# A two-block transformer kernel: norms without GpSimd, and the second block's edges done stream by stream

## The chip, the cores and the metric

The kernel runs on one core of a Trainium2 chip. The metric is device time in microseconds (us), the median of several executions. A core has a matrix engine (TensorE, PE in the profile), three engines for elementwise work (VectorE or DVE, ScalarE or ACT, GpSimd or POOL) and a queue that issues transfers (SyncE or SP). Each engine executes its instructions in the order in which they were laid down when the kernel was built, and waits at an instruction until what it needs is there.

## The reference

Two blocks follow each other. The first works on 256 tokens of 1024 features: a gated FFN, an attention mixer, another gated FFN, each between two RMS norms. The second has two streams, the 256 tokens x and 256 context tokens xc, and two layers. All is float32. Cut to what matters:

```python
def rms_norm(x, g):
    return x * lax.rsqrt(jnp.mean(x * x, axis=-1, keepdims=True) + EPS) * g

def adaln_norm(x, g, shift, scale):
    return rms_norm(x, g) * (1 + scale) + shift

# first block
x = x + 0.5 * rmsnorm(swiglu(rmsnorm(x, ffn1_pre_g), ...), ffn1_post_g)
x = x + rmsnorm(mixer(rmsnorm(x, mix_pre_g)), mix_post_g)
x = x + 0.5 * rmsnorm(swiglu(rmsnorm(x, ffn2_pre_g), ...), ffn2_post_g)

# second block, layer l; mx and mc are six vectors each, from a small matmul (modulation)
h, hc = adaln_norm(x, norm1_g[l], mx[0], mx[1]), adaln_norm(xc, norm1_g[l], mc[0], mc[1])
# three branches (Fourier, window attention, gated scan) of h @ w_in[l] and hc @ w_in[l]
if not last:
    xc = xc + mc[2] * yc                  # yc = merged branches @ w_out[l]
    xc = xc + mc[5] * sq_relu_mlp(adaln_norm(xc, norm2_g[l], mc[3], mc[4]), w_ff1[l], w_ff2[l])
x = x + mx[2] * y
x = x + mx[5] * sq_relu_mlp(adaln_norm(x, norm2_g[l], mx[3], mx[4]), w_ff1[l], w_ff2[l])
```

In the last layer the context is needed only for keys, values and states, so only x has outputs there.

## The kernel before, in words

Features lie on partitions, eight tiles of 128, and tokens along the free axis. Each float32 operand of a matmul is split into a high and a low part, and each product is three matmuls (`mm3`, L239 to L242). A weight comes in units of 512 KB (`wunit`, L230): a DMA into `raw`, a cast on ScalarE for `hi` (L235), a subtraction on VectorE for `lo` (L236), with three buffers each. `linear` (L246) makes 256 output features from units of four input tiles. In the first block it is 256 tokens wide, so a unit feeds 24 matmuls of 256 columns; in the second block's layer 0 both streams go together in 512 columns.

A norm's sum of squares is gathered by `Sums` (L316): each output block is squared on ScalarE, the squares of the blocks but the last are added on GpSimd (L341), and matmuls with one column (`tok`, L323) sum over the features, for the added squares when the block before the last has come (L343 to L345), for the last one at the end. The row scales come from a few small steps (`rs_tok`, L360, a power on GpSimd) and are spread over all partitions by two diagonal tiles and two matmuls with them (`spread`, L369). `post_norm` (L421) scales the outputs and adds them to X, the second of four pairs on GpSimd (L437); `pre_norm` (L411) then splits X times gain into high and low parts (`gained`, L394) and makes the next sums. While a norm waits, PE does fillers: columns of the second block's gates for the context (`ctx_gate`, L702).

`adaln` (L448) is the norm of the second block. It takes both streams at once where there are two. For each of eight k: a multiplication on VectorE (L458), per stream an Identity with scale and bias on ScalarE for `hi` (L461) and a multiply-add on GpSimd (L462), and a subtraction on VectorE for `lo` (L465). It stands in the prologue for the context, beside FFN2 for the context, at the start of layer 0 for x, between w_out and ff1 of each layer, and between the layers.

In `layer` (L885) the two streams' outputs of w_out come block by block of 256 features, four blocks; `residual` adds them to x (L1335), the squares of the last block go in halves (`half`, L350). Then adaln, then ff1 in two halves of the hidden features, each followed by ff2. `mods` (L663), the modulation matmuls of layer 1 with their transfers of 1 MB, are handed out between these by `next(between)`. After the branches' projections, `hcol(0)` makes the first head's forget columns and its query and gate, `values` the value columns for both streams, `scan(0)` the first head's gated scan. The order on each engine is set by a scheduler at build time, which goes by priorities; nothing in it is written out by hand.

## Time and profile before

| | |
|---|---|
| median of three runs | 2115.73 us (2113.39 to 2123.27) |
| the profiled execution | 2119.52 us, span 2117.7 us |
| mean granted clock of TensorE | 0.985 |
| busy: PE, VectorE, ScalarE, GpSimd | 97%, 59%, 49%, 8% |

The times of one profiled execution are used throughout; it took 3.8 us more than the median. PE's busy time is the sum of its matmuls' durations, which overlap in a pipeline, so a busy PE is not PE at its peak: what a matmul takes is read from the distance of two starts, or from a count in a window. The granted clock of a window is 1.00 at full speed (2.4 GHz) and 0.50 at the lower level (1.2 GHz).

### The profile page before, as it was taken

The page shows a single profiled execution, that of the slowest core. Times are in us where ns is not written, and L with a number is a line of the kernel's source. Part 1 is how long each engine was busy: PE and PEld are TensorE (multiplying, and loading weights), DVE is VectorE, ACT ScalarE, POOL GpSimd, SP SyncE. Part 2 cuts the span into 40 slices and gives each one's busy share as a digit, 9 for nine tenths or more (in the row PEclk, how much of TensorE's full clock was granted, in tenths as well). Part 3 has the DMA queues.
Part 4 walks back from the last instruction along what each step waited for, and adds up shares of the span by engine and source line. Part 5 has one row for each costly group of instructions (what it writes and reads, how often), then busy time and mean ns, then how long its engine had stood idle before and what let it go on. Part 6 is the DMA issues. An engine that isn't in the chain of part 4 may idle for free.

```text
span 2117.7 us, 33603 instructions
## 1 busy us (share of the span) xinstructions
PE 2056.8 (97%) x13623; PEld 1795.5 (85%) x13623; DVE 1259.8 (59%) x1930; ACT 1047.0 (49%) x1692; POOL 159.6 (8%) x154
## 2 busy tenths in 40 slices
PE   8999999999999999999999999999999998998999
PEld 8899988999999777888776678778778778998998
DVE  5574666765557699855454442343267897666644
ACT  5353455544446688655343331233255776555532
POOL 1131110211220000000002000000120000001000
PEclk9999999999999999999999999999999999999999
DMA  7986564566552211168533663342233223654654
GB/s 231 304 241 188 174 169 131 158 186 181 173 194 81 70 40 50 53 223 273 193 131 106 212 225 129 110 149 90 86 104 90 61 63 108 211 178 143 187 186 135
DMA packets 284158, 318.57 MB, mean 150 GB/s; under 512 B 18528, under 2 KB 272306, under 8 KB 277346
## 3 DMA queue, kind: packets, MB, share of 16 engines
q1 hardware_dynamic: 284002, 316.42, 47.8%
q8 instruction: 107, 1.75, 0.3%
q14 instruction: 49, 0.40, 0.1%
HBM read 308.96 MB, written 11.35 MB: 151 GB/s over the span
## 4 chain that ended last, share of the span: by engine, by line
PE 89%; DVE 4%; ACT 4%; POOL 2%; issue 1%; DMA 1%; SPq 0%; POOLq 0%; DVEq 0%; ACTq 0%
PE mx L240 13%; PE mx L242 13%; PE mx L241 13%; PE mm L240 11%; PE mm L242 11%; PE mm L241 11%; PE hg L1168 2%; POOL sq L462 1%; PE ax L326 1%; PE mx L674 1%; PE ax L674 1%; PE at L1029 1%; PE at L1066 1%; DVE lo L236 1%; PE at L1056 1%
## 5 line engine op out<-in xcount | busy, mean ns | idle before, releaser
L236 DVE TENSOR_TENSOR lo<-raw,hi 128x1024 fp32r<-128x1024 f32 x460 | 563.5, 1226 | 564.3 <-ACT hi L235 558.2
L235 ACT CAST hi<-raw 128x1024 fp32r<-128x1024 f32 x460 | 478.3, 1040 | 742.9 <-PE mx L241 417.5
L240 PE MATMUL mx<-hh,hi 128*128 128x256 f32 (+1 forms) x1216 | 377.3, 310 | 4.3 <-ACT hh L461 3.0
L241 PE MATMUL mx<-hl,hi 128*128 128x256 f32 (+1 forms) x1216 | 374.8, 308 | 3.0 <-DVE hl L465 2.4
L242 PE MATMUL mx<-hh,lo 128*128 128x256 f32 (+1 forms) x1216 | 375.2, 309 | 1.7 <-DVE lo L236 1.7
L240 PE MATMUL mm<-hh,hi 128*128 128x256 f32 (+1 forms) x1096 | 363.6, 332 | 2.0 <-ACT z L1111 1.3
L242 PE MATMUL mm<-hh,lo 128*128 128x256 f32 (+1 forms) x1096 | 360.1, 329 | 0.0
L241 PE MATMUL mm<-hl,hi 128*128 128x256 f32 (+1 forms) x1096 | 358.1, 327 | 1.1 <-DVE hl L465 1.0
L240 PEld LDWEIGHTS mx<-hh,hi 128*128 128x128 f32 x1216 | 231.3, 190 | 29.8 <-ACT hi L235 6.7
L241 PEld LDWEIGHTS mx<-hl,hi 128*128 128x128 f32 x1216 | 232.2, 191 | 18.4 <-DVE hl L465 6.0
L242 PEld LDWEIGHTS mx<-hh,lo 128*128 128x128 f32 x1216 | 230.7, 190 | 13.2 <-DVE lo L236 1.9
L240 PEld LDWEIGHTS mm<-hh,hi 128*128 128x128 f32 x1096 | 208.8, 191 | 28.1 <-issue 5.8
L241 PEld LDWEIGHTS mm<-hl,hi 128*128 128x128 f32 x1096 | 209.3, 191 | 18.9 <-issue 2.5
L242 PEld LDWEIGHTS mm<-hh,lo 128*128 128x128 f32 x1096 | 208.3, 190 | 16.8 <-issue 2.3
L240 PE MATMUL mx<-fh,hi 128*128 128x512 f32 (+1 forms) x288 | 100.3, 348 | 0.0
L241 PE MATMUL mx<-fl,hi 128*128 128x512 f32 (+1 forms) x288 | 100.2, 348 | 0.0
L242 PE MATMUL mx<-fh,lo 128*128 128x512 f32 (+1 forms) x288 | 100.0, 347 | 0.0
L341 POOL TENSOR_TENSOR acc<-sq 128x512 f32<-128x512 f32 x12 | 20.3, 1690 | 872.9 <-ACT sq L331 872.9
L242 PE MATMUL mm<-fh,lo 128*128 128x256 f32 (+1 forms) x224 | 74.7, 333 | 0.0
L240 PE MATMUL mm<-fh,hi 128*128 128x256 f32 (+1 forms) x224 | 74.3, 332 | 0.0
L241 PE MATMUL mm<-fl,hi 128*128 128x256 f32 (+1 forms) x224 | 74.1, 331 | 0.0
L242 PE MATMUL mx<-hidh,lo 128*128 128x256 f32 x220 | 62.4, 283 | 0.7 <-DVE lo L236 0.7
(373 smaller groups left out, 3864.5 us busy)
## 6 DMA issues: line engine op xcount, KB each, us to landing
raw<-in_w_ff_dram SPq DMA_DIRECT2D x128, 512.0 KB
raw<-in_w_in_dram SPq DMA_DIRECT2D x124, 512.0 KB
wm<-in_w_mod_dram SPq DMA_DIRECT2D x48, 1024.0 KB
raw<-in_ffn_w_gate_dram SPq DMA_DIRECT2D x44, 512.0 KB
raw<-in_ffn_w_up_dram SPq DMA_DIRECT2D x44, 512.0 KB
raw<-in_ffn_w_down_dram SPq DMA_DIRECT2D x40, 512.0 KB
raw<-in_w_qkv_dram SPq DMA_DIRECT2D x24, 512.0 KB
raw<-in_w_out_dram SPq DMA_DIRECT2D x24, 512.0 KB
```

Of the source, the lines that this page charges most:

```text
L235: S.copy(hi, raw)
L236: V.tensor_tensor(out=lo, in0=raw, in1=hi.bitcast(F32), op=ALU.subtract)
L240: PE.matmul(ps, l[0], r[0], start=start, stop=False)
L241: PE.matmul(ps, l[0], r[1], start=False, stop=False)
L242: return PE.matmul(ps, l[1], r[0], start=False, stop=stop)
L326: PE.matmul(self.ss[:, t:t + 1], sq[:, i * T + t * P:i * T + (t + 1) * P], ones[:, :1], start=(first and i == 0 and t == 0), stop=(last an ...
L462: nc.gpsimd.tensor_scalar(out=xs, in0=xs, scalar1=A[s][:, k:k + 1], scalar2=B[s][:, k:k + 1], op0=ALU.mult, op1=ALU.add)
L674: PE.matmul(ps[32 * c:32 * c + 32, :], cst_[:, k, :], wm[:, c * 512:(c + 1) * 512], start=(k == 0), stop=(k == KD - 1), tile_position=(0, ...
L1029: PE.matmul(scs[t], q[e][:, t * P:(t + 1) * P], kd[g][i][:, 512 - nk:], start=(i == 0), stop=(i == 1 and s == 1))
L1056: PE.transpose(pt[:, kt * T + t * P:kt * T + (t + 1) * P], sb[:, c0:c0 + P], ident)
L1066: mm = PE.matmul(op[e * 64:e * 64 + 64, :T], vt[:, vc:vc + 64], pts[e][:, kt * T:(kt + 1) * T], start=(ki == 0), stop=(ki == nk // P - 1))
L1168: PE.matmul(ps[:, (s * 2 + st) * P:(s * 2 + st + 1) * P], kt[:, s * T + st * P:s * T + (st + 1) * P], qt[:, s * T + tt * P:s * T + (tt + 1 ...
```

## The change

Four things are changed.

- **Sums.** The additions of squares go to VectorE, and the one-column matmuls for the added squares are issued with the last block (in `half`, with its first half). The second pair's addition to X in `post_norm` goes to VectorE too.
- **Gained inputs.** `post_norm` can make the next norm's gained parts right after each pair of X.
- **adaln.** It goes stream by stream inside k: VectorE multiplies x by the scale and the row factor, ScalarE adds the bias for `hi`, VectorE adds the bias and subtracts `hi` for `lo`. GpSimd keeps the power of the row scales.
- **Streams.** In layer 0, blocks 2 and 3 of w_out are done for the context, then for x, each followed by its adaln; the first two blocks of ff1 in the same way; so is the last block of the second ff2, followed by layer 1's adaln of that stream. Layer 1 starts with the context's part of the first head's forget columns and the context's values (`values1`), then x's part and x's values. Weight units that are used for each stream apart are fetched, cast and split twice: 18 units more.

```diff
     class Sums:
...
                 elif self.j < self.n - 1:
                     acc = tmp(512, "acc", 2) if self.j == 1 else self.acc
-                    nc.gpsimd.tensor_tensor(out=acc, in0=self.acc, in1=sq, op=ALU.add)
+                    V.tensor_tensor(out=acc, in0=self.acc, in1=sq, op=ALU.add)
                     self.acc = acc
-                if self.j == self.n - 2:
+                if self.j == self.n - 1:
                     self.ss = ax_tile()
                     self.tok(self.acc, True, False)
-                if self.j == self.n - 1:
                     self.tok(sq, False, True)
...
             S.activation(sq, src, AF.Square)
+            if i == 0:
+                self.ss = ax_tile()
+                self.tok(self.acc, True, False)
...
-    def pre_norm(g, ss=None):
-
-        units = [gained(lambda i: X[:, 2 * j + i, 0, :], g + 2 * j, *pair(j)) for j in range(4)]
+    def gained_x(g, j):
+        return gained(lambda i: X[:, 2 * j + i, 0, :], g + 2 * j, *pair(j))
...
-    def post_norm(pss, g, factor, fill=()):
+    def post_norm(pss, g, factor, fill=(), then=None):
...
                 V.tensor_tensor(out=two(hs[j]), in0=two(hs[j]), in1=twice(rs), op=ALU.mult)
-                (nc.gpsimd if j == 1 else V).tensor_tensor(out=xpair(j), in0=two(hs[j]), in1=xpair(j), op=ALU.add)
+                V.tensor_tensor(out=xpair(j), in0=two(hs[j]), in1=xpair(j), op=ALU.add)
+                if then is not None:
+                    units.append(gained_x(then, j))
+        return units
...
         for k in range(KD):
-            hi, lo = units[k]
-            xn = tmp(512, "sq", 3)[:, c]
-            V.tensor_tensor(out=xn, in0=x[:, k, s0:s1, :].rearrange("p s t -> p (s t)"), in1=ps[:, c], op=ALU.mult)
             for s in streams:
-                xs = xn[:, (s - s0) * T:(s - s0 + 1) * T]
-                S.activation(hi[:, s * T - at:(s + 1) * T - at], xs, AF.Identity, scale=A[s][:, k:k + 1], bias=B[s][:, k:k + 1])
-                nc.gpsimd.tensor_scalar(out=xs, in0=xs, scalar1=A[s][:, k:k + 1], scalar2=B[s][:, k:k + 1],
-                                        op0=ALU.mult, op1=ALU.add)
-            cu = slice(s0 * T - at, s1 * T - at)
-            V.tensor_tensor(out=lo[:, cu], in0=xn, in1=hi[:, cu].bitcast(F32), op=ALU.subtract)
+                hi, lo = (u[:, s * T - at:(s + 1) * T - at] for u in units[k])
+                u = tmp(512, "sq", 3)[:, :T]
+                V.scalar_tensor_tensor(out=u, in0=x[:, k, s, :], scalar=A[s][:, k:k + 1], in1=ps[:, s * T:(s + 1) * T],
+                                       op0=ALU.mult, op1=ALU.mult)
+                S.activation(hi, u, AF.Identity, bias=B[s][:, k:k + 1])
+                V.scalar_tensor_tensor(out=lo, in0=u, scalar=B[s][:, k:k + 1], in1=hi.bitcast(F32),
+                                       op0=ALU.add, op1=ALU.subtract)
...
+        def values1(s):
+
+            for b in range(2):
+                if s == 1:
+                    vh.append([None, None])
+                [ps] = linear_tok(w_in, 0, KD, C_I + b * 256, of(hboth, s), T)
+                vh[b][s] = ut("vh", 4)
+                V.tensor_copy(vh[b][s], ps)
...
-        hcol(0)
-        values()
+        if last:
+
+            early = [linear128(w_in, c, hboth, 512, ((1, "at"),)) for c in (C_FF, C_FB)]
+            values1(1)
+            hcol(0, early)
+            values1(0)
+        else:
+            hcol(0)
+            values()
...
-        for jb in range(4):
+
+        for jb in range(4 if last else 2):
             residual(linear(a["w_out_2"][l], 0, KD, jb * 256, mact, ntok), jb, 2, sums)
+        if not last:
+            h = mh
+            for s in (1, 0):
+                for jb in (2, 3):
+                    [ps] = linear(a["w_out_2"][l], 0, KD, jb * 256, of(mact, s), T)
+                    residual1(ps, jb, 2, s, sums)
+                adaln(x, (s,), A2, B2, h, sums)
...
-            for j in range(n_h):
+            if hf == 0 and not last:
...
+                for s in (1, 0):
+                    for j in range(2):
+                        [ps] = linear(a["w_ff1_2"][l], 0, KD, j * 256, of(hboth, s), T)
+                        next(between, None)
...
-            for jb in range(4):
+            for jb in range(4 if last or hf == 0 else 3):
                 residual(linear(a["w_ff2_2"][l], hf * kh * P, kh, jb * 256, fact, ntok), jb, 5,
                          sums if hf == ns - 1 else None)
...
+            h1 = [pair(k) for k in range(KD)]
+            for s in (1, 0):
+                [ps] = linear(a["w_ff2_2"][l], kh * P, kh, 3 * 256, of(fact, s), T)
+                residual1(ps, 3, 5, s, sums)
+                adaln(x, (s,), [derived[l + 1][q][0] for q in range(2)], [modt[l + 1][:, q, 0:8] for q in range(2)], h1, sums)
```

`residual1` does for one stream what `residual` does for both, and `of(act, s)` takes a stream's columns of the operands.

How this moves instructions is seen at three places. The first is the end of FFN1 on PE, where the down projection's third block ends. In a row the names are output, stationary and moving operand, then the tile; `ax` is the tile of the sum, `acc` the added squares, `hid` the hidden features. Before:

```order
L241 MATMUL mx<-hidl,hi 128x256
L242 MATMUL mx<-hidh,lo 128x256
L326 MATMUL ax<-cmain,acc 128x1 x4
L240 MATMUL mx<-hidh,hi 128x256
L241 MATMUL mx<-hidl,hi 128x256
```

And now, at the end of the fourth block, with the filler (`hch`, `hcl`, the context's parts) behind it:

```order
L242 MATMUL mx<-hidh,lo 128x256
L326 MATMUL ax<-cmain,acc 128x1 x4
L240 MATMUL mm<-hch,hi 128x256
L241 MATMUL mm<-hcl,hi 128x256
L242 MATMUL mm<-hch,lo 128x256
```

The matmuls that read the added squares moved behind the fourth block, 114 rows later on PE.

The second place is PE between w_out and ff1 of layer 0. `sq` is the last block's square, `wm` a modulation weight, `diag` the diagonal tile, `hh` and `hl` the norm's high and low parts. Before:

```order
L242 MATMUL mx<-hh,lo 128x512
L355 MATMUL ax<-cmain,sq 128x1 x4
L674 MATMUL mx<-wm,csil_12035 32x512 x5
L355 MATMUL ax<-cmain,sq 128x1 x4
L674 MATMUL mx<-wm,csil_12035 32x512 x3
L379 MATMUL ax<-diag,cmain 128x128 x4
L240 MATMUL mx<-hh,hi 128x512
L240 MATMUL mm<-hh,hi 128x512
L674 MATMUL mx<-wm,csil_12035 32x512
L241 MATMUL mx<-hl,hi 128x512
```

And now the context's spread, between two matmuls of w_out's blocks for x:

```order
L240 MATMUL mm<-hh,hi 128x256
L241 MATMUL mm<-hl,hi 128x256
L381 MATMUL ax<-diag,cmain 128x128 x2
L242 MATMUL mm<-hh,lo 128x256
L240 MATMUL mm<-hh,hi 128x256
```

The matmuls with the diagonals no longer stand right ahead of the first matmul that reads the norm's output; the other stream's matmuls lie around them.

The third place is VectorE at the same edge. `big` is the residual x, `rvs` the row sums, `der` and `modt` the scale and the shift. Before:

```order
L236 TENSOR_TENSOR lo<-raw,hi 128x1024 x2
L1335 SCALAR_TENSOR_TENSOR big<-mm,modt_139,big 128x256 x2
L1335 SCALAR_TENSOR_TENSOR big<-mx,modt_139,big 128x256 x2
L236 TENSOR_TENSOR lo<-raw,hi 128x1024
L363 TENSOR_SCALAR rvs<-ax 128x2 x2
L376 TENSOR_SCALAR diag<-cmain,rss 128x128 x2
L458 TENSOR_TENSOR sq<-big,ax 128x512 x3
L465 TENSOR_TENSOR hl<-sq,hh 128x512
L458 TENSOR_TENSOR sq<-big,ax 128x512
L465 TENSOR_TENSOR hl<-sq,hh 128x512 x2
```

And now, for the context, up to x's turn:

```order
L365 TENSOR_SCALAR rvs<-ax 128x2
L378 TENSOR_SCALAR diag<-cmain,rss 128x128
L469 SCALAR_TENSOR_TENSOR sq<-big,der_144,ax 128x256 x3
L472 SCALAR_TENSOR_TENSOR hl<-sq,modt_139,hh 128x256 x3
L469 SCALAR_TENSOR_TENSOR sq<-big,der_144,ax 128x256 x3
L1374 SCALAR_TENSOR_TENSOR big<-mm,modt_139,big 128x256
L472 SCALAR_TENSOR_TENSOR hl<-sq,modt_139,hh 128x256 x3
L469 SCALAR_TENSOR_TENSOR sq<-big,der_144,ax 128x256 x2
L1374 SCALAR_TENSOR_TENSOR big<-mm,modt_139,big 128x256
L236 TENSOR_TENSOR lo<-raw,hi 128x1024
L472 SCALAR_TENSOR_TENSOR hl<-sq,modt_139,hh 128x256 x2
L341 TENSOR_TENSOR acc<-acc,sq 128x512
```

The norm's steps come in threes for one stream, with x's residuals, a weight's low part and an addition of squares between them.

## Rows read from the trace of the kernel before

**Rows 1.** Page: busy time and share of each engine; traffic in 40 slices, GB/s

```profile
PE 2056.8 (97%) x13623; PEld 1795.5 (85%) x13623; DVE 1259.8 (59%) x1930; ACT 1047.0 (49%) x1692; POOL 159.6 (8%) x154
...
GB/s 231 304 241 188 174 169 131 158 186 181 173 194 81 70 40 50 53 223 273 193 131 106 212 225 129 110 149 90 86 104 90 61 63 108 211 178 143 187 186 135
```

**Rows 2.** Page: the chain of work that ended last, by engine

```profile
PE 89%; DVE 4%; ACT 4%; POOL 2%; issue 1%; DMA 1%; SPq 0%; POOLq 0%; DVEq 0%; ACTq 0%
```

**Rows 3.** PE's waits over the span: us in total, times, longest

```profile
PE ax L326 <- POOL acc L341: 7.7, 6, 1.5
...
PE ax L379 <- DVE diag L376: 3.6, 5, 1.4
...
PE mx L240 <- ACT hh L461: 3.0, 2, 1.9
...
PE mx L241 <- DVE hl L465: 2.4, 4, 1.0
...
PE mx L242 <- DVE lo L236: 2.3, 2, 1.7
...
PE at L240 <- ACT hh L461: 1.9, 1, 1.9
...
PE ax L355 <- ACT sq L353: 1.4, 1, 1.4
```

**Rows 4.** Nine windows: engines' busy us (instructions), granted clock, DMA share, GB/s

```profile
209.09:212.50 3.41, 3.41 (x17) 3.41 (x18) 0.29 (x1) 1.04 (x1) 0.00 (x0) 0.50 0.27 75
...
1134.10:1140.93 6.83, 6.83 (x23) 5.77 (x23) 0.00 (x0) 0.00 (x0) 0.40 (x1) 0.50 0.17 60
...
1919.17:1929.41 10.24, 7.45 (x31) 6.87 (x32) 6.23 (x17) 4.88 (x9) 5.88 (x9) 0.50 0.18 53
sum 51.20, PE 47.58 PEld 43.28 DVE 17.00 ACT 14.22 POOL 16.49; mean PE 5.29 PEld 4.81 DVE 1.89 ACT 1.58 POOL 1.83
```

**Rows 5.** Timeline, 205.5 to 210 us: start, duration, instruction

```profile
206.68 1.75 POOL L341 TENSOR_TENSOR acc<-acc,sq 128x512 f32<-128x512 f32 x1 [13.67 <-ACT sq L331]
...
206.92 0.28 PE L242 MATMUL mx<-hidh,lo 128*128 128x256 f32 x1
...
208.48 1.34 PE L326 MATMUL ax<-cmain,acc 128*128 128x1 f32 x8 [1.27 <-POOL acc L341]
```

**Rows 6.** Instructions by line and shape: busy us, mean ns, idle before

```profile
L236 DVE TENSOR_TENSOR lo<-raw,hi 128x1024 fp32r<-128x1024 f32 x452 | 558.0, 1236 | 557.2 <-ACT hi L235 551.0 <-PE ax L982 4.3
...
L399 DVE SCALAR_TENSOR_TENSOR hl<-big,vec,hh 128x256 fp32r<-128x256 f32 x24 | 13.9, 651 | 0.0
...
L399 DVE SCALAR_TENSOR_TENSOR hl<-o,vec,hh 128x256 fp32r<-128x256 f32 x8 | 3.9, 485 | 4.6 <-ACT hh L398 4.6
L437 DVE TENSOR_TENSOR big<-h,big 128x512 f32<-128x512 f32 x6 | 3.9, 683 | 0.0
...
L462 POOL TENSOR_SCALAR sq<-sq,der,modt 128x256 f32<-128x256 f32 x64 | 49.1, 777 | 27.7 <-ACT hh L461 22.6 <-ACT hch L461 5.0
...
L341 POOL TENSOR_TENSOR acc<-acc,sq 128x512 f32<-128x512 f32 x12 | 18.0, 1508 | 60.3 <-ACT sq L331 60.1
```

**Rows 7.** Windows as in rows 4, steady stretches and edges

```profile
160.00:200.00 40.00, 40.00 (x344) 40.00 (x343) 19.56 (x19) 15.70 (x18) 5.03 (x3) 1.00 0.66 197
578.00:592.00 14.00, 12.72 (x108) 12.51 (x107) 6.73 (x6) 4.69 (x5) 1.74 (x1) 1.00 0.47 146
1110.00:1120.00 10.00, 10.00 (x44) 8.07 (x43) 3.25 (x6) 2.41 (x3) 0.00 (x0) 1.00 0.34 107
1152.00:1171.00 19.00, 14.80 (x58) 9.26 (x56) 13.11 (x19) 10.14 (x20) 13.03 (x17) 1.00 0.36 131
1551.00:1572.00 21.00, 16.53 (x62) 11.49 (x62) 13.00 (x25) 9.59 (x19) 12.85 (x18) 0.84 0.27 89
```

**Rows 8.** VectorE's timeline from 239.2 us

```profile
238.80 3.75 DVE L399 SCALAR_TENSOR_TENSOR hl<-big,vec,hh 128x256 fp32r<-128x256 f32 x4
```

More of the change, by code (lines that the diff above doesn't have):

```diff
@@ L409, in row_scale, with pre_norm @@
         return col, row
-    def pre_norm(g, ss=None):
-        units = [gained(lambda i: X[:, 2 * j + i, 0, :], g + 2 * j, *pair(j)) for j in range(4)]
+    def gained_x(g, j):
+        return gained(lambda i: X[:, 2 * j + i, 0, :], g + 2 * j, *pair(j))
+    def pre_norm(g, ss=None, units=None):
+        if units is None:
+            units = [gained_x(g, j) for j in range(4)]
         if ss is None:
@@ L432, in post_norm @@
             f()
+        units = []
         with tc.high_priority(offset=200):
@@ L487, in pinned, with ffn @@
             yield
-    def ffn(pre, w_gate, w_up, w_down, post, between, ss=None, middle=None, fill=()):
-        xn, _, rs = pre_norm(pre, ss)
+    def ffn(pre, w_gate, w_up, w_down, post, between, ss=None, units=None, middle=None, fill=(), then=None):
+        xn, _, rs = pre_norm(pre, ss, units)
         act = unit_act(xn)
@@ L517, in ffn @@
             middle()
-        post_norm(down(), post, 0.5, fill)
-        return last
+        return last, post_norm(down(), post, 0.5, fill, then)
     rel_d = dp.tile([120, P], F32, name="rel_d")
@@ L588, in heads, with mixer @@
         V.tensor_copy(oj[:, i * T:(i + 1) * T], op[:, :T])
-    def mixer(between, fill):
-        xn, rs_col, rs = pre_norm(V_MIXPRE)
+    def mixer(between, fill, units):
+        xn, rs_col, rs = pre_norm(V_MIXPRE, None, units)
         act = unit_act(xn)
@@ L784, in blocks_kernel @@
     between = prologue()
-    last = ffn(V_F1PRE, a["ffn1_w_gate"][0], a["ffn1_w_up"][0], a["ffn1_w_down"][0], V_F1POST, between, x_rs,
-               fill=gates[:3])
+    last, units = ffn(V_F1PRE, a["ffn1_w_gate"][0], a["ffn1_w_up"][0], a["ffn1_w_down"][0], V_F1POST, between, x_rs,
+                      fill=gates[:3], then=V_MIXPRE)
     for _ in between:
@@ L790, in blocks_kernel @@
     with pinned(last):
-        mixer(between, gates[3:6])
+        units = mixer(between, gates[3:6], units)
     wide[0] = "mx"
@@ L799, in ctx_norm @@
         adaln(X, (1,), (None, derived[0][1][0]), (None, modt[0][:, 1, 0:8]), h0, {1: sums_of(X, 1, True)})
-    last = ffn(V_F2PRE, a["ffn2_w_gate"][0], a["ffn2_w_up"][0], a["ffn2_w_down"][0], V_F2POST, between,
-               middle=ctx_norm, fill=gates[6:])
+    last, _ = ffn(V_F2PRE, a["ffn2_w_gate"][0], a["ffn2_w_up"][0], a["ffn2_w_down"][0], V_F2POST, between,
+                  units=units, middle=ctx_norm, fill=gates[6:])
     b1.close()
@@ L883, in sigmoid_, with layer @@
         S.activation(e, e, AF.Exp, scale=-1.0)
-    def layer(l, x, sums):
+    def layer(l, x, h):
         last = l == 1
@@ L898, in layer, with of @@
         if l == 0:
-            h = h0
             adaln(x, (0,), A1, B1, h, {0: sums_of(x, 0, False)})
             constants()
-        else:
-            h = [pair(k) for k in range(KD)]
-            adaln(x, (1, 0), A1, B1, h, sums)
         nc.sync.dma_start(out=xd, in_=x.rearrange(flat))
+        def of(act, s):
+            return lambda k: tuple(u[:, s * T:(s + 1) * T] for u in act(k))
         def hboth(k):
@@ L1134, in layer, with hcol @@
         hin = {}
-        def hcol(hd):
+        def hcol(hd, early=None):
             gt = ut("gt", 2, 2048)
@@ L1341, in residual, with residual1 @@
                     sums[s].add(pair_of(x, jb, s))
+        def residual1(ps, jb, i, s, sums):
+            for n in range(2):
+                k = jb * 2 + n
+                V.scalar_tensor_tensor(out=x[:, k, s, :], in0=ps[:, n * T:(n + 1) * T], scalar=m(s, i)[:, k:k + 1],
+                                       in1=x[:, k, s, :], op0=ALU.mult, op1=ALU.add)
+                if jb == 3:
+                    sums[s].half(x[:, k, s, :], n)
+            if jb < 3:
+                sums[s].add(pair_of(x, jb, s))
         streams = tuple(range(ns))
         sums = {s: Sums(4) for s in streams}
-        for jb in range(4):
+        for jb in range(4 if last else 2):
             residual(linear(a["w_out_2"][l], 0, KD, jb * 256, mact, ntok), jb, 2, sums)
+        if not last:
[5 more added lines that the diff above has]
+                adaln(x, (s,), A2, B2, h, sums)
         fp = fs.enter_context(tc.tile_pool(name=f"ff{l}", bufs=1, reuse_waits="tile"))
@@ L1352, in layer @@
             next(between, None)
-        h = [pair(k) for k in range(KD)]
-        adaln(x, streams, A2, B2, h, sums)
+        if last:
+            h = [pair(k) for k in range(KD)]
+            adaln(x, streams, A2, B2, h, sums)
         sums = None if last else {s: Sums(4) for s in streams}
```

40 lines of the change are left out of this document (28 added, 12 removed).

## The prediction

> **What bounds the kernel now.** I read the page first. TensorE (PE) is busy for 2056.8 us, 97% of the span, and the chain that ended last is PE for 89% [rows 1, 2]. No other engine is near its limit on average (VectorE 59%, ScalarE 49%, GpSimd 8%), so only time that PE loses counts, and the second view, PE's waits by line and releaser, tells who takes it. The largest entry is the sum of squares waiting for an add on GpSimd: 7.7 us in 6 waits. The rest of what the change touches are the diagonal tile of a norm (3.6), the first norm outputs (3.0 and 1.9), their low parts (2.4), a weight's low part (2.3) and one square (1.4) [rows 3]: together 22.3 us idle.
>
> The third view is the granted clock in windows. Behind these waits PE runs in stretches at 0.50, the lower level of 1.2 GHz. The nine stretches that lie at places of this change add up to 51.2 us, in which PE is busy for 47.6; at the upper level that work would take half, so the clock costs up to 23.8 us (three of them and the sum stand in [rows 4]). One place in a timeline shows both: a matmul starts at 206.92, the next at 208.48, released by GpSimd's add of 206.68 to 208.43; one matmul's usual 0.12 off, that is 1.44 us, and from 209.09 the clock is at half for 3.41 us, worth 1.7 [rows 4, 5]. Start to start a wait costs somewhat more than its idle time, since the pipeline refills; I added up start-to-start excesses at all these places by hand and have some 56 us, 2.6% of the run. That is all the change can win.
>
> **Sums of squares.** The 24 adds go from GpSimd (1.5 us or more each) to VectorE, where an add of this shape takes 0.68 [rows 6]; and the matmuls that read the sum are issued with the last element, behind another whole output block (over 100 matmuls of 0.116 us, more than 11 us) [rows 7]. So the add may queue behind several casts' low parts of 1.24 us and still be early: the cover is the last output block. All six waits go: 6 x 1.4 = 8.4 us. The clock stretches that follow four of them (3.41, 3.41, 6.83, 6.83) are worth half, 10.2. I take all of it: 18 us. VectorE pays 24 x 0.68 = 16 us for it, at places where it is at about half load [rows 7].
>
> **Norm edges of the first block.** Gained inputs now follow each X pair at once, and VectorE's two-operand steps lose the neighbour on GpSimd that stretched them: the same step takes 0.65 on average in the norms beside GpSimd's adds, 0.485 elsewhere [rows 6]. At the edge from mixer to FFN2 this ends the longest wait for a diagonal (1.4), and the stretch of 3.41 behind it, worth 1.7; the two waits for a weight's low part behind the context's norms (2.3) go too, since no GpSimd step holds VectorE's queue there any more [rows 3, 6]. Against that, in VectorE's new order a weight's low part stands behind gained steps at the mixer's start, and I expect a new wait of about 1.0, one low part of 1.24. At the start of the second block waits for norm low parts shrink, and about as much comes back at the row-scale chain, whose power function still runs on GpSimd: 0 to 2, I take 0.6. 1.4 + 1.7 + 2.3 - 1.0 + 0.6 = 5 us.
>
> **The norm of each stream (adaln).** A step of one k was a 512-wide multiply on VectorE, two Identity on ScalarE, two multiply-adds on GpSimd (0.78 each) and a subtraction; now it is, per stream, one VectorE step, one Identity and one VectorE step, 256 wide, 0.485 each [rows 6]. The 64 GpSimd instructions go (49.1 us of that engine), no wait on GpSimd stays inside the loop. On VectorE 32 steps for two streams cost 32 x 0.485 = 15.5 us, against 16 steps of 512 at about 0.68, 10.9: 4.6 more.
>
> GpSimd's step on one operand takes 0.777 and VectorE's 0.485 [rows 6]. The Trainium skill (GPSIMD Engine Reference, Engine selection) says that for one-input elementwise work GpSimd is at roughly VectorE's pace, which speaks against this part: by it the exchange would leave the waits for norm low parts as they were, and the time would come out 2.4 us later, at 2091. The row disagrees, by a factor of 1.6.
>
> **Stream by stream.** Layer 0's w_out blocks 2 and 3, the first two ff1 blocks and the last ff2 block are done 256 wide, context first, and each stream's norm lies beside the other stream's matmuls. Before, PE is idle for 4.2 of the 19 us from 1152 to 1171, and for 4.5 of 21 us at the edge between the layers [rows 7]. What hides the norm now: 96 matmuls per stream, 96 x 0.116 = 11.2 us, and at the second edge the context's forget columns and values. The cost has three parts. A split matmul: two at 0.1163 against one at 0.2273 (10 us over 44), so 336 x 0.005 = 1.8 us. Weights read twice: 18 units more of 512 KB, one cast and one low part each, 18 x 1.24 = 22 us of VectorE, beside matmuls that take 24 x 0.116 = 2.8 us per unit. And new waits: VectorE is nearly full there. Per stretch it has 16 low parts (19.8), 32 norm steps (15.5) and some 9 of residuals, adds and squares: 44 us against about 52 of PE (four times 11.2, and 16 modulation matmuls). The order shows PE waiting for low parts queued behind norm steps once, about 2 us, and some half-microsecond waits for diagonals: 3.2 at the first edge, 3 to 5 at the second. Start to start, the excess beside the sums is 5.8 at the first edge and some 8.3 at the second, clock apart (the idle time and its refills); so the win is about 2.6 + 4.3 = 7, with 3.4 of clock at the second: 10. In layer 1's own middle there is one stream; the sum's wait is counted above, the square's (1.4) is partly covered by the moved matmuls, the chain and the first outputs stay: 2 us.
>
> DMA: the stream-wise ff1 asks for 8 units of 0.52 MB and 4 modulation tiles of 1.05 MB, 8.4 MB, in about 30 us, 280 GB/s; 304 is seen in the page's second slice, where PE is not short of weights [rows 1]. I cost it at nothing. If it did not hold, it would cost a few us.
>
> **Sum.** 18 + 5 + 10 + 2 - 1.8 = 33 us. I take 5 off, for each new wait of the three edges may bring a stretch at half clock as the old ones did (3.41, worth 1.7) [rows 4], and 1 for layer 1's forget chain, which now has one stream's values as cover, about 11 us, instead of two. That leaves 27: 2119.5 (the profiled execution, span 2117.7) becomes 2092. The median shown is 3.8 below the profiled execution, so about **2089 us**, 1.3% faster.
>
> **Rivals.** *Everything goes:* waits and clock both, 56 - 1.8 = 54 us, 2062. For it: in steady stretches the clock is 1.00 without a break [rows 7]. Against: the row-scale chain and the first outputs in layer 1 have no cover, and VectorE is full at the edges. *The waits go, the clock stretches stay:* each edge still has narrow matmuls, 8 of one column and 4 of the diagonal, and PE falls back behind any of them; then the 14 us of clock in my sum are missing, 27 - 14 = 13 us, 2103. For it: the stretches of rows 4 follow waits of 1.5 us and less. Against: in the window from 578 to 592 PE waits for GpSimd's add as elsewhere, and the clock stays at 1.00 [rows 7]. *VectorE becomes the bound (slower):* the norm steps of the stream-wise stretches run at 0.94 instead of 0.485, as the worst four do beside a GpSimd add today (3.75 us) [rows 8]. Then 32 steps take 30, a stretch holds 59 us of VectorE against 52 of PE: 7 late, twice, 8 more in layer 1, and with PE starved a stretch at half clock at each of five norms (3.4 each, 17): 39 us. Against it stand the sums and the first block alone, 18 + 5 - 2 = 21: 18 slower, about 2134. It decides from a step of about 0.75. Against: nothing but power functions of two columns is left on GpSimd. *The order undoes the change:* VectorE executes in order, and a sum's add stands behind three low parts; were the sums' matmuls waiting for it, nothing of the 18 would come and the time be 2107. The place of the matmuls speaks against it.
>
> **How the numbers follow.** Forecast (2075 to 2100): 0.58. Everything: 0.12. Clock stays or the order undoes half: 0.22, of which half within 0.5% of the median (10.6 us, about what a measurement here can tell from no change). Slower by VectorE: 0.05, and 0.03 for a win that ends at nothing. So faster 0.81, same 0.14, slower 0.05. The range, 2066 to 2109, takes in the forecast, half of the first rival and most of the second.
>
> **What would show it.** Right: no wait of PE on L341; no POOL instruction in the adaln loop; adaln's steps on VectorE at 0.4 to 0.5; the stretches at 0.50 near 209, 383, 1134 and 1523 gone; PE busy above 95% in the two edges; fewer idle microseconds at the diagonals. Wrong: norm steps above 0.7, PE waiting for L236 in the stream-wise stretches for more than 5 us, or clock stretches of the old length at the new places.

## The result, and the profile after

The changed kernel takes 2091.08 us (median; 2090.21 to 2092.26), the kernel before 2115.38 beside it: a ratio of 0.9879, 95% interval 0.9853 to 0.9904. Forecast were 2089 and a range of 2066 to 2109. The profiled execution took 2091.31 us, 28 less than that of before.

The page of the changed kernel, the lines that answer to [rows 1, 2]:

```profile
span 2089.2 us, 34286 instructions
...
PE 2039.9 (98%) x13959; PEld 1802.4 (86%) x13959; DVE 1292.0 (62%) x2011; ACT 1060.4 (51%) x1716; POOL 69.4 (3%) x63
...
PE 91%; DVE 3%; ACT 3%; DMA 1%; issue 1%; POOL 0%; SPq 0%; POOLq 0%; DVEq 0%; ACTq 0%
```

VectorE has 32 us more work and GpSimd 90 less. PE's waits over the span, the answer to [rows 3] (lines have moved: L381 is the diagonal's matmul, L471 and L472 the norm's high and low part, L352 the square):

```profile
PE ax L381 <- DVE diag L378: 4.2, 7, 1.4
...
PE ax L357 <- ACT sq L352: 2.6, 2, 2.0
...
PE mx L242 <- DVE lo L236: 2.0, 3, 1.4
...
PE mm L242 <- DVE lo L236: 1.5, 2, 0.8
...
PE mm L240 <- ACT hh L471: 1.1, 1, 1.1
...
PE mm L241 <- DVE hl L472: 0.3, 1, 0.3
```

No wait for a sum is left, 1.1 of the 4.9 us for first outputs and 0.3 for norm low parts. The square has 2.6 instead of 1.4, and the diagonals have more than before. (For low parts [rows 3] shows 2.4, into one tile; the waits into the other two add 1.0 and 0.9, so 4.3 fell to 0.3.) VectorE's steps by shape, as in [rows 6]:

```profile
L469 DVE SCALAR_TENSOR_TENSOR sq<-big,der,ax 128x256 f32<-128x256 f32 x64 | 27.3, 474 | 8.2 <-PE ax L381 8.2
L472 DVE SCALAR_TENSOR_TENSOR hl<-sq,modt,hh 128x256 fp32r<-128x256 f32 x56 | 24.5, 480 | 1.0 <-ACT hh L471 0.8
...
L401 DVE SCALAR_TENSOR_TENSOR hl<-big,vec,hh 128x256 fp32r<-128x256 f32 x24 | 10.1, 480 | 0.1
...
L341 DVE TENSOR_TENSOR acc<-acc,sq 128x512 f32<-128x512 f32 x12 | 8.1, 684 | 0.0
```

The gained step (X and the high part are its two inputs) fell from 651 to 480 ns, with no add on GpSimd beside it. The Trainium skill (SBUF — State Buffer, Who interferes with whom) says that a VectorE instruction with two inputs in SBUF contends with a GpSimd instruction that reads there; the fall agrees.

Windows in the changed kernel, columns as in [rows 4]: two stretches at 0.50, the sum of six, and the two edges with layer 1's middle:

```profile
1530.82:1534.23 3.41, 3.41 (x18) 3.41 (x18) 1.58 (x3) 0.40 (x1) 0.69 (x1) 0.50 1.16 380
...
1892.63:1899.46 6.83, 5.34 (x22) 4.91 (x23) 5.48 (x15) 3.01 (x7) 0.00 (x0) 0.50 0.25 74
sum 34.12, PE 30.71 PEld 26.64 DVE 24.68 ACT 16.89 POOL 2.37; mean PE 5.12 PEld 4.44 DVE 4.11 ACT 2.81 POOL 0.39
...
1110.00:1160.00 50.00, 48.34 (x387) 42.35 (x386) 35.61 (x65) 24.98 (x43) 1.38 (x2) 1.00 0.67 219
1500.00:1575.00 75.00, 71.56 (x583) 70.60 (x580) 55.39 (x95) 42.55 (x73) 1.38 (x2) 0.98 0.57 173
1885.00:1900.00 15.00, 11.88 (x77) 11.28 (x76) 10.65 (x22) 6.23 (x12) 0.69 (x1) 0.77 0.41 127
```

The stretches at 209, 246, 383, 403 and 1134 are gone; the two from 1523 and 1557, 13.66 us, have become one of 3.41. At the edges PE is busy for 97% and 95%, and VectorE for 71% and 74%.

Where the time went is read from the same events in both traces (the difference is after minus before, added up from the start):

| event | before, us | after, us | difference |
|---|---|---|---|
| first score matmul of the mixer | 264.9 | 261.7 | -3.2 |
| first scan matmul of layer 0 | 665.3 | 652.8 | -12.4 |
| last modulation matmul ahead of layer 0's w_out | 1072.8 | 1060.2 | -12.6 |
| first modulation matmul of the second ff1 half | 1368.3 | 1348.0 | -20.2 |
| first scan matmul of layer 1 | 1600.7 | 1571.4 | -29.3 |
| last scan matmul of layer 1 | 1780.6 | 1753.1 | -27.5 |
| last matmul | 2113.5 | 2084.8 | -28.6 |

So 12.4 us come from the first block and the second's start, 7.6 from layer 0's edge, 9.1 from the edge between the layers, and layer 1 gives 0.7 back.

For the experiments the clock is taken apart from the rest: I add up the stretches at 0.50 in each profile (from 100 us to the last matmul), take half as what they cost, and call the time of the last matmul less that half the rest.

| kernel | last matmul | at 0.50 | clock's cost | rest |
|---|---|---|---|---|
| before | 2113.5 | 64.9 | 32.4 | 2081.1 |
| changed | 2084.8 | 34.1 | 17.1 | 2067.8 |
| e_place | 2101.4 | 61.4 | 30.7 | 2070.7 |
| e_engine | 2093.6 | 41.0 | 20.5 | 2073.1 |
| e_sums | 2097.3 | 54.6 | 27.3 | 2070.0 |
| e_adaln | 2110.8 | 61.4 | 30.7 | 2080.1 |
| e_no_streams | 2094.5 | 51.2 | 25.6 | 2068.9 |
| e_streams_pool | 2095.3 | 41.0 | 20.5 | 2074.8 |
| e_no_early | 2086.2 | 44.4 | 22.2 | 2064.0 |
| e_no_ff1 | 2081.3 | 30.7 | 15.4 | 2066.0 |
| e_less | 2084.0 | 37.6 | 18.8 | 2065.2 |

Of the 28.6 us 15.3 are clock. Each is one execution, and the stretches in layer 1's attention (10.24 or 13.65 us) differ between kernels that are the same there, so a difference of 3 us in the clock column says little. The stretch of 3.41 near 246 shows it too: it is gone in the changed kernel, and back near 244 in e_no_ff1, e_less and e_filler, whose order on PE is the same as the changed kernel's up to there.

### The profile page after: what moved, and what is told of

It is laid out like the page before. It is cut to its first block, busy times and chain, and to the rows that moved or that the text cites. A ratio compares the mean times of both kernels' runs of the same rounds, so it can differ in the third digit from the quotient of the medians.

```text
span 2089.2 us, 34286 instructions
## 1 busy us (share of the span) xinstructions
PE 2039.9 (98%) x13959; PEld 1802.4 (86%) x13959; DVE 1292.0 (62%) x2011; ACT 1060.4 (51%) x1716; POOL 69.4 (3%) x63
## 4 chain that ended last, share of the span: by engine, by line
PE 91%; DVE 3%; ACT 3%; DMA 1%; issue 1%; POOL 0%; SPq 0%; POOLq 0%; DVEq 0%; ACTq 0%
PE mx L240 14%; PE mx L242 14%; PE mx L241 14%; PE mm L240 12%; PE mm L242 12%; PE mm L241 12%; PE hg L1187 2%; PE ax L681 1%; PE at L1036 1%; PE ax L326 1%; PE mx L681 1%; PE at L1073 1%; PE at L1063 1%; PE at L240 1%; PE at L242 1%; PE at L241 1%
## 5 line engine op out<-in xcount | busy, mean ns | idle before, releaser
L236 DVE TENSOR_TENSOR lo<-raw,hi 128x1024 fp32r<-128x1024 f32 x478 | 584.8, 1225 | 511.0 <-ACT hi L235 507.0
L235 ACT CAST hi<-raw 128x1024 fp32r<-128x1024 f32 x478 | 497.3, 1041 | 716.1 <-PE mx L241 390.7
L240 PE MATMUL mx<-fh,hi 128*128 128x256 f32 (+1 forms) x368 | 120.3, 327 | 0.0
L241 PE MATMUL mx<-fl,hi 128*128 128x256 f32 (+1 forms) x368 | 120.3, 327 | 0.0
L242 PE MATMUL mx<-fh,lo 128*128 128x256 f32 (+1 forms) x368 | 120.2, 327 | 0.0
L240 PEld LDWEIGHTS mx<-fh,hi 128*128 128x128 f32 x368 | 69.2, 188 | 6.8
L241 PEld LDWEIGHTS mx<-fl,hi 128*128 128x128 f32 x368 | 69.2, 188 | 6.6
L242 PEld LDWEIGHTS mx<-fh,lo 128*128 128x128 f32 x368 | 69.4, 188 | 6.4
L1187 PE MATMUL hg<-qt,kt 128*128 128x128 f32 x384 | 62.0, 285 | 1.0 <-ACT dg L1194 0.5
L1187 PEld LDWEIGHTS hg<-qt,kt 128*128 128x128 f32 x384 | 55.2, 197 | 7.7 <-issue 2.1
```

The costliest lines, as they stand in the source:

```text
L235: S.copy(hi, raw)
L236: V.tensor_tensor(out=lo, in0=raw, in1=hi.bitcast(F32), op=ALU.subtract)
L240: PE.matmul(ps, l[0], r[0], start=start, stop=False)
L241: PE.matmul(ps, l[0], r[1], start=False, stop=False)
L242: return PE.matmul(ps, l[1], r[0], start=False, stop=stop)
L1187: PE.matmul(ps[:, (s * 2 + st) * P:(s * 2 + st + 1) * P], kt[:, s * T + st * P:s * T + (st + 1) * P], qt[:, s * T + tt * P:s * T + (tt + 1 ...
```

## The experiments

### The sums: place, engine, both

e_place, on the kernel before:

```diff
-                if self.j == self.n - 2:
+                if self.j == self.n - 1:
                     self.ss = ax_tile()
                     self.tok(self.acc, True, False)
-                if self.j == self.n - 1:
                     self.tok(sq, False, True)
...
+            if i == 0:
+                self.ss = ax_tile()
+                self.tok(self.acc, True, False)
```

> The kernel before, in which only the place of the one-column matmuls is changed: those that read the added squares are issued with the last output block; the adds stay on GpSimd. Theory (the place heals the sums, since an add of 1.5 to 1.75 us has over 11 us of matmuls as cover there): no wait of PE on L341 is left, about 15 us less than before, 2100 us. Rival (the engine counts: GpSimd's adds are long and stretch VectorE's steps): at most 5 us less, 2110.

e_engine, on the kernel before; e_sums is both edits:

```diff
-                    nc.gpsimd.tensor_tensor(out=acc, in0=self.acc, in1=sq, op=ALU.add)
+                    V.tensor_tensor(out=acc, in0=self.acc, in1=sq, op=ALU.add)
```

> The kernel before, in which only the engine of the adds is changed, VectorE for GpSimd; the one-column matmuls stay with the third block. Theory (the place counts): PE still waits at the sum, for the square (0.6 us) and an add of 0.68 queued on VectorE behind a low part of 1.24, so the six waits shrink by a third at most and their clock stretches stay; 2 to 5 us less for the stretched steps alone, 2112 us. Rival (the engine counts): 12 us less or more, 2103.

> The kernel before with both parts of the change to the sums, place and engine. The prediction's term is 18 us with its clock, and with the stretched steps at the edge of mixer and FFN2 (wait and clock, 3.1) some 20: 2096 us. If VectorE's 16 us of adds cost something where they stand, less than e_place gains.

Measured: e_place 2107.17 us, ratio 0.9941 (0.9922 to 0.9960); e_engine 2100.55, 0.9915 (0.9891 to 0.9939); e_sums 2104.07, 0.9930 (0.9906 to 0.9955). So 12, 18 and 15 us, and the rival won on e_engine, the engine alone does it all; in e_place the theory came close, 12 of 15. There is no wait on L341 in e_engine either; e_sums has one of 0.6 us. Two timelines around the first sum, VectorE's and PE's:

```profile
207.71 1.23 DVE L236 TENSOR_TENSOR lo<-raw,hi 128x1024 fp32r<-128x1024 f32 x1 [0.19 <-ACT hi L235]
208.86 0.69 DVE L341 TENSOR_TENSOR acc<-acc,sq 128x512 f32<-128x512 f32 x1
...
209.60 1.05 PE L326 MATMUL ax<-cmain,acc 128*128 128x1 f32 x8
```

The add ends at 209.55, later than GpSimd's did in [rows 5], and PE does not wait. The add is 0.69 us long instead of 1.75, and the one-column matmuls stand six rows later in PE's order than before. That order is the scheduler's; that it took GpSimd's add for shorter than it is would explain the old place, but no run shows it.

In e_place one wait is left, at the mixer's end. PE's waits from 360 to 392 us, GpSimd's timeline, and PE's:

```profile
PE ax L326 <- POOL acc L341: 1.5, 1, 1.5
...
373.81 1.51 POOL L341 TENSOR_TENSOR acc<-acc,sq 128x512 f32<-128x512 f32 x1 [1.36 <-ACT sq L331]
...
375.38 1.05 PE L326 MATMUL ax<-cmain,acc 128*128 128x1 f32 x8 [1.54 <-POOL acc L341]
```

There the last block is one weight unit, 24 matmuls or 2.8 us, not 11, as I had taken it to be everywhere. And the edit of the place moved nothing there: in the kernel before, too, the matmuls for the added squares stand behind all four blocks and 18 matmuls of fillers, five rows ahead of the last square's (380.53 and 382.11 us there, 375.38 and 376.97 here). So the place healed five of the six waits, and the mixer's went with the engine.

e_engine also shows what healed the edge behind the mixer. With only the adds' engine changed, the gained step of that kernel takes this:

```profile
L399 DVE SCALAR_TENSOR_TENSOR hl<-big,vec,hh 128x256 fp32r<-128x256 f32 x24 | 9.8, 477 | 0.0
```

The wait for the mixer's diagonal is 0.3 us instead of 1.3 there, and the stretch at 403 is gone. No run has the gained inputs alone, so what they give is not shown. Layer 0's first scan matmul comes 3.9 us earlier in e_no_streams than in e_sums, and the norm's form, which is in that difference too, brings it 2.4 us forward by itself in e_adaln.

Without the clock e_place and e_sums are better than e_engine (2070.7, 2070.0, 2073.1); the clock turns it around, and not in one execution alone: the mean granted clock was 0.990 to 0.992 in e_engine's four runs and 0.986 to 0.988 in e_sums's four. The intervals of their times overlap all the same. The timeline of PE in e_sums at layer 0's edge, rows that stand for several instructions:

```profile
1131.62 0.95 PE L326 MATMUL ax<-cmain,acc 128*128 128x1 f32 x8
1132.43 0.58 PE L357 MATMUL ax<-cmain,sq 128*128 128x1 f32 x4
1132.88 1.03 PE L326 MATMUL ax<-cmain,acc 128*128 128x1 f32 x8
1133.77 0.58 PE L357 MATMUL ax<-cmain,sq 128*128 128x1 f32 x4
1134.28 2.93 PE L676 MATMUL mx<-wm,csil 128*32 128x512 f32 x10
1137.15 1.87 PE L357 MATMUL ax<-cmain,sq 128*128 128x1 f32 x8
1138.94 1.93 PE L676 MATMUL mx<-wm,csil 128*32 128x512 f32 x6
1140.80 2.57 PE L381 MATMUL ax<-diag,cmain 128*128 128x128 f32 x8
1145.28 0.80 PE L240 MATMUL mx<-hh,hi 128*128 128x512 f32 x1 [1.91 <-ACT hh L463]
```

The late place gathers both streams' one-column matmuls ahead of modulation and diagonals, and from 1135.02 the clock is at 0.50 for 13.65 us, though PE is not idle until 1143. In e_engine, with the added squares' matmuls inside the blocks, the only stretch there is 3.41 from 1141.13, behind the wait for hh.

The gathered matmuls alone do not decide it, though. PE's order in e_no_streams (below) is the same through all of them and for over 2700 matmuls ahead of them, and at the edge between the layers both kernels have such a row again, also in the same order. Windows over the row, columns as in [rows 4], e_sums first, then e_no_streams:

```profile
1131.62:1143.37 11.75, 11.72 (x57) 7.00 (x55) 2.92 (x7) 2.55 (x5) 1.42 (x2) 0.64 0.39 118
1530.29:1539.78 9.49, 8.43 (x61) 5.65 (x59) 3.90 (x12) 2.58 (x5) 1.38 (x2) 1.00 0.78 276
...
1127.67:1135.93 8.26, 8.03 (x57) 5.26 (x55) 2.96 (x7) 2.56 (x5) 1.34 (x2) 1.00 0.45 141
1520.69:1533.75 13.06, 12.23 (x61) 7.68 (x59) 3.95 (x12) 2.58 (x5) 1.38 (x2) 0.64 0.57 202
```

In e_sums the clock falls at the first edge and holds at the second (1.00), in e_no_streams it holds at the first and falls at the second. What decides stays open.

### The form of the norm

e_adaln puts the new `adaln`, as in the change, into the kernel before; e_streams_pool puts the old one into the changed kernel.

> The kernel before with the norm of the second block in the new form (two VectorE steps and an Identity per stream, nothing on GpSimd but the power), both streams together as before, sums as before. Theory: the steps take 0.48 against GpSimd's 0.78, PE's waits for norm low parts (2.4 us in 4) go and those for the first outputs (4.9) stay or fall a little, 3 us less: 2112 us. Rival (a one-input step is no slower on GpSimd, and VectorE has more to do): no difference, 2115, with the waits for low parts as they were.

> The changed kernel, the norm of the second block in the old form with GpSimd's multiply-add, stream by stream. Theory: 8 steps of 0.78 on GpSimd are 6.2 us per stream, and the other stream's matmuls (11.2 us) hide them, so only layer 1's middle, with one stream, loses: 2 to 3 us more, 2094 us. Rival (GpSimd beside VectorE stretches VectorE's steps, which are full in these stretches): 8 us more, 2099.

Measured: e_adaln 2114.33 us, 0.9981 (0.9967 to 0.9995), 4 us (its waits for norm low parts are gone, and PE waits 2.2 and 0.8 us for two low parts of weights instead); e_streams_pool 2101.64, 0.9925 (0.9902 to 0.9949), 10 us more than the changed kernel by the ratios. The rival's size came, not its mechanism. The steps of VectorE and GpSimd in e_streams_pool:

```profile
L477 DVE TENSOR_TENSOR hl<-sq,hh 128x256 fp32r<-128x256 f32 x56 | 25.1, 448 | 17.1 <-POOL sq L474 16.5
L470 DVE TENSOR_TENSOR sq<-big,ax 128x256 f32<-128x256 f32 x64 | 24.1, 416 | 8.0 <-PE ax L381 7.9
...
L1056 DVE TENSOR_SCALAR sb<-sb,den 128x256 f32<-128x256 f32 x16 | 4.9, 348 | 0.0
...
L474 POOL TENSOR_SCALAR sq<-sq,der,modt 128x256 f32<-128x256 f32 x64 | 54.7, 863 | 40.4 <-ACT hh L473 32.2 <-ACT hch L473 5.0 <-PE at L242 3.2
```

VectorE's steps are as short as ever. But VectorE stands idle for 16.5 us waiting for GpSimd's step, and as it works in order, the residuals and low parts behind it are late: PE waits 4.3 us at once for the square at the edge between the layers, 1.8 for a sum's add and 1.4 for a low part. GpSimd's one-input step takes 863 ns here; VectorE's two-input step, which took its place, takes 480 in the changed kernel, and a one-input step of this shape on VectorE 348 (L1056, from the attention). So the Trainium skill's statement (GPSIMD Engine Reference, Engine selection) that one-input work on GpSimd is at about VectorE's pace does not hold for this shape.

### The streams, whole and in parts

e_no_streams has `layer` and what it calls as before, with the new sums, gained inputs and norm. e_no_early and e_no_ff1 take one part out, e_less both:

```diff
         if last:
-
-            early = [linear128(w_in, c, hboth, 512, ((1, "at"),)) for c in (C_FF, C_FB)]
-            values1(1)
-            hcol(0, early)
-            values1(0)
-        else:
-            hcol(0)
-            values()
+        hcol(0)
+        values()
...
-            if hf == 0 and not last:
+            if False:
```

> The changed kernel with the layers' order of before: w_out, ff1, ff2 and the norms with both streams together, no weight read twice; sums, gained inputs and the new form of the norm are kept. Theory: the two edges lose what the streams gave, 7 us by the prediction's terms and 3.4 of clock at the second edge, and win back the split matmuls (1.8): 9 us more than the changed kernel, 2100 us. Rival (what made the edges short was the sums and the norm's form, and the streams only pay for themselves): 2092 or less.

> The changed kernel, in which layer 1 starts as before, with the forget columns for both streams at once and the values after them. The norm of x at the edge between the layers then has nothing beside it. Theory: PE waits for the row-scale chain and the first outputs of x's norm there (2.1 and more, with a clock stretch), 6 us more, and wins back about 1 in the scan's start: 2096 us. Rival (the edge's norm is hidden by the last ff2 block alone): 2090.

> The changed kernel, in which the first two ff1 blocks take both streams at once, 512 columns wide, so 8 units of weights fewer are read; w_out stays stream by stream. Theory: the norm of x has no other stream's matmuls beside it but modulation, PE waits for its chain and first outputs, 4 us, possibly a clock stretch, less about 0.5 for splitting and VectorE's 10 us: 2095 us. Rival (x's norm is quick enough with VectorE freed of 8 low parts): 2090.

> The changed kernel without two of its parts that cost nothing when taken out alone: ff1 takes both streams at once, and layer 1 starts as before. Only w_out's last two blocks and the last ff2 block go stream by stream (8 units of weights read twice instead of 18). Theory (with these two parts out, VectorE has 12 us of low parts less, and w_out's and ff2's own other stream hides the context's norm, which is all that the streams give): 2087 to 2091 us, no slower than the changed kernel. Rival (the parts stand in for each other, and without both x's two norms lie bare): 2097, like the kernel with no streams at all.

Measured: e_no_streams 2098.00 us, 0.9899 (0.9873 to 0.9926); e_no_early 2092.65, 0.9876 (0.9853 to 0.9900); e_no_ff1 2089.91, 0.9865 (0.9841 to 0.9888); e_less 2090.89, 0.9868 (0.9852 to 0.9885). The changed kernel has 0.9879. (Stream-wise ff1 reads four units twice, not the eight that its expectation says.) So the streams together give about 4 us by the ratios, but the intervals overlap: that they give anything is likely, not shown. Stream-wise ff1 and the early start of layer 1 give nothing that these times show, and the kernel without both is as fast with 10 units of weights fewer to read twice.

The profiles say why. In e_no_streams PE waits for the norm at the first edge, from 1120 to 1185 us, and at the second, from 1505 to 1580:

```profile
PE mx L240 <- ACT hh L471: 1.5, 1, 1.5
PE ax L381 <- DVE diag L378: 0.2, 1, 0.2
...
PE mm L241 <- DVE lo L236: 2.2, 1, 2.2
PE at L240 <- ACT hh L471: 1.5, 1, 1.5
```

and at the second edge three more of 0.8 to 1.1. Its waits for hl are gone, by the norm's form alone, and the rest is only 1.1 us above the changed kernel's. What the streams win at the second edge is clock: 17.07 and 6.83 us at 0.50 there in e_no_streams, 3.41 in the changed kernel. This is one execution of each, and part of it may be chance, since the same row of matmuls kept the full clock in e_sums. Over all four runs the mean granted clock is 0.9893 in e_no_streams and 0.9908 in the changed kernel, which makes some 3 us of 2090, an estimate, against 8.5 in the table. At the first edge the streams give little: from the last modulation matmul ahead of w_out to the first of the second ff1 half it is 295.5 us before, 288.6 in e_no_streams and 287.9 in the changed kernel.

The early start does cover x's norm: without it, in e_no_early, PE waits 2.0 us for the diagonal and 1.1 for the first outputs, with 10.24 us at 0.50, as the theory said. The kernel makes up for it elsewhere; its rest in the table is 3.8 us lower than the changed kernel's. And the streams have waits of their own, as at 1527 in the changed kernel, where VectorE, ScalarE and PE stand so:

```profile
1524.57 1.21 DVE L236 TENSOR_TENSOR lo<-raw,hi 128x1024 fp32r<-128x1024 f32 x1
...
1528.03 1.04 ACT L235 CAST hi<-raw 128x1024 fp32r<-128x1024 f32 x1 [2.44 <-DMA raw<-in_w_in_dram]
1528.98 0.72 ACT L352 ACTIVATE sq<-big 128x256 f32<-128x256 f32 x2
...
1529.44 0.61 PE L357 MATMUL ax<-cmain,sq 128*128 128x1 f32 x4 [2.02 <-ACT sq L352]
```

A low part ends at 1525.78, then its buffer is free and the next transfer is issued (1525.85); the cast of that waits for it, and the square that PE waits for stands behind the cast.

### VectorE as the bound, and two attempts to do better

e_double issues each of the norm's two VectorE steps twice. e_lo200 wraps the weights' low parts in `tc.high_priority(offset=200)`. e_filler adds 12 and 9 matmuls of 256 columns, whose result is not used, behind the sums and the diagonals of layer 1's middle.

> The changed kernel, in which both VectorE steps of the second block's norm are issued twice (the second writes the same values again), so a step costs 0.95 us instead of 0.48: the slower rival of the prediction, made on purpose. By its price (14 us of VectorE over its cover in the two edges, 8 in layer 1's middle, a stretch at half clock at each of five norms, 17): 39 us more than the changed kernel, 2130 us. Against that, the low parts that the waiting PE doesn't ask for meanwhile give VectorE time, and the extra steps at the edges are partly hidden still: 15 us more, 2106.

> The changed kernel, in which the weights' low parts have a higher priority in the scheduler, so that they stand ahead of norm and gained steps on VectorE. Theory (late low parts hold the weight buffers, so the next transfer, the cast behind it and the square behind the cast come late): the waits for low parts at the mixer's start (1.4) and in ff1 (0.7) and the 2.0 for the square at the edge between the layers with its clock stretch go, 5 us less, 2086 us. Rival (VectorE is full in these stretches, so what low parts gain the norm's steps lose): 2091 or more, with waits for hh and hl instead.

> The changed kernel, with 21 matmuls of 256 columns in layer 1's middle whose result nobody reads: 12 between the one-column matmuls and the diagonal ones, 9 behind these, where PE idles for 1.4 and 1.1 us. Nothing else is changed. Theory (the clock falls there because PE idles): the stretch of 6.83 us at half clock behind this norm goes, 3 us less, 2088 us. Rival (the narrow matmuls or the wait for the square ahead of them bring it down): the stretch stays, 2091.

Measured: e_double 2142.76 us, 1.0108 (1.0079 to 1.0137), 48 us more than the changed kernel and slower than before: the slower rival's price of 39 was, if anything, low. PE's waits in e_double:

```profile
PE mx L242 <- DVE lo L236: 10.4, 5, 8.2
PE mx L683 <- DMA wm<-in_w_mod_dram: 8.8, 3, 3.5
PE ax L357 <- ACT sq L352: 6.6, 3, 5.6
```

The largest single wait (8.2) is in the prologue's norm, which I had left out of the price; modulation's transfers (8.8 us), which I read as late behind weights that wait for buffers, are a second thing that it did not have. Of the 52 us between the two profiles' last matmuls 17.9 lie ahead of layer 0's first scan matmul (670.7 against 652.8), where the price had only clock.

e_lo200: 2107.65, 0.9952 (0.9937 to 0.9966), 16 us worse than the changed kernel. The rival's time came, and worse: no low part is waited for, but what is pulled ahead on VectorE pushes something else back, not hh and hl, as it had said, but the scans and the attention (PE's longest entries there are 5.0 us for `z` and 4.2 for `sb`, against 1.7 and 1.1 in the changed kernel). It changed the order everywhere, so it does not tell whether the late transfer makes the wait at 1527; that stays a reading of the trace.

e_filler: 2091.67, 0.9869 (0.9844 to 0.9895), no difference. PE's timeline in it:

```profile
1891.27 1.05 PE L357 MATMUL ax<-cmain,sq 128*128 128x1 f32 x8 [0.59 <-ACT sq L352]
1892.19 2.74 PE L467 MATMUL mm<-hh 128*128 128x256 f32 x12
1894.73 1.05 PE L383 MATMUL ax<-diag,cmain 128*128 128x128 f32 x4
1895.43 1.49 PE L467 MATMUL mm<-hh 128*128 128x256 f32 x9
1897.69 0.38 PE L240 MATMUL mm<-hh,hi 128*128 128x256 f32 x1 [0.76 <-ACT hh L484]
```

The clock fell at 1892.39 all the same, just as the fillers began: what brings it down lies ahead of them. They ran at half speed, 2.5 us instead of the 1.4 that were idle, and held the diagonals back. The stretch shrank from 6.83 to 3.41 us, and the 1.7 so won were lost again.

## Why the prediction was right, point by point

The total was right (27 forecast, 28 measured), and where the time came from was nearly right by place: for the first block and the second's start my terms add up to 12.6 (three sums 4.2, their clock 3.4, the norm edges 5), measured 12.4. For the two edges they are 14.5 after the discount (sums 2.8, their clock 6.8, streams 10, less 1.8 and two thirds of the 5), measured 16.7; for layer 1 about +0.7, measured -0.7. By mechanism it was less so, and that the total came out so close is in part luck: terms that were too large and gains that the sum did not have nearly cancel. Of the rivals, the one that the clock stretches stay is ruled out by the table (64.9 us at 0.50 before, 34.1 now).

- **Sums.** 18 forecast, 15 measured in e_sums. The waits (8.4) are right but for one of 0.6: the rest falls by 11, stretched steps included. The clock term (10.2) was too large for this edit alone, 5.1 in its profile, where the gathered narrow matmuls ran at 0.50 for 13.65 us at one edge; that they need not, e_no_streams shows. In the whole change the clock gave 15.3, in all places together. The step that failed is the reason: "the matmuls that read the sum are issued with the last element" was to be what heals, with over 11 us of cover. The engine alone heals as much, and at the mixer the edit of the place moved nothing; the sixth wait stayed in e_place.
- **Norm edges of the first block.** As forecast in size: the mixer's diagonal (1.3 before; the 1.4 of the prediction is layer 1's) and the stretch behind it are gone, the new wait at the mixer's start is 1.4 for 1.0, and the two for weights' low parts behind the context's norms (2.3) are down to 0.4, as in e_adaln. But the diagonal and its stretch go with the adds' engine alone (e_engine), so of the two reasons given, the lost neighbour on GpSimd is shown and the gained inputs are not. The stretch at 246, which I had left standing, went too, by chance: three kernels with the same code there have it.
- **The norm's form.** Forecast 2.4 to 3, measured 4 alone, but 10 within the streams: the two parts need each other, which the sum of separate terms could not show. What I had set GpSimd's one-input step (777 ns) against was a two-input step of VectorE (485); a one-input step of that shape takes VectorE 346 in the kernel before (L1045), so GpSimd is slower by a factor of 2.2, not 1.6.
- **Streams.** The step "the win is about 2.6 + 4.3 = 7, with 3.4 of clock" was wrong in its split: about 1 us of waits and some 8 of clock in the profiles, 4 us by the times. I had put the loss of the edges down to missing cover; at the first edge 6.9 of the 7.6 us come without the streams, by the sums and the norm's form. Two of the four parts that go stream by stream, ff1 and layer 1's start, give nothing by the times.
- **VectorE.** No new wait on L236 above 1.4 at the edges, as forecast (0.7 and 0.8), and the rival's price had about the right size when it was made to come true, in part for other reasons. The transfers, which I had costed at nothing, cost 0.3 us of wait at the first edge. The deduction of 5 for new clock stretches came as 1.7 at 1530, beside what is left of the old ones.
- **Diagonals.** I said their idle time would fall; it rose from 3.6 to 4.2. The one at layer 1's middle (1.4) stayed, and one of 1.2 at the second block's start is new, at the row-scale chain, as forecast there.
- **Layer 1.** From the last scan matmul on 1.2 us were gained, for 2 and the sum's 1.4: the sum's wait went and the square's fell from 1.4 to 0.6, but the chain and the first outputs stayed (1.4 and 1.1), and waits of 1.3 for a cast and 0.8 for a low part are new. The branch phase lost 1.8, for 1; it has 17.1 us at 0.50 instead of 10.2, so without the clock it lost nothing.

## What to carry to other kernels

Work on a slow engine costs less by its own time than by what stands behind it in order: GpSimd's adds cost 18 us of waits and clock in a kernel where GpSimd is 8% busy, and its step in the middle of a VectorE chain cost 4 us in the kernel before and 10 with the streams. Do such engine changes first and measure them, before restructuring for more cover; here the streams, with all their code, added some 4 of the 25 us, and not even that is sure. And when two profiles differ in their stretches at half clock, look for the same matmuls in a third before giving the difference to the edit.

## What the runs showed of the hardware

TensorE's clock fell without idle time. In e_sums PE ran one-column, 32-row and 128-column matmuls without a gap from 1131.62 to 1143, and the granted clock was 0.50 from 1135.02 for 13.65 us. In e_engine the same matmuls with eight fewer of one column per stream in that place came through at 1.00 up to 1141. But the full row came through at 1.00 as well, at the same edge in e_no_streams (1127.67 to 1135.93) and at the other edge in e_sums itself (1530.29 to 1539.78); so such a row can go with a fall and need not, and no run here shows what decides.

A filler that starts with the fall does not undo it: in e_filler the clock fell 0.2 us after the fillers began, and 3.41 us at half clock remained.
